# First stage of a hybrid encoder layer: x loaded first, modulation sums of the first block on TensorE, later sums spread

## The chip, the cores and the metric

The kernel runs on one core of one Trainium2 chip. The metric is the device time of one execution in microseconds (us), the median of several runs. Each engine (TensorE = PE with its weight loads PEld, VectorE = DVE, ScalarE = ACT, GpSimd = POOL, SyncE = SP) works through its own queue in order.

## The reference, cut to what matters

One encoder layer, 512 positions by 2048 features, float32. What bears on the change is its first step:

```python
c_act = silu(c)                                  # 2048 values
mod = c_act @ w_ada[l] + b_ada[l]                # w_ada: 2048 x 12288
sh1, sc1, gt1, sh2, sc2, gt2 = split(mod, 6)
h = rms_norm(x, g_norm1[l]) * (1 + sc1) + sh1    # 512 x 2048
proj = h @ w_in[l]
...
```

After it come two kinds of attention, an output projection, a second modulated norm and a SwiGLU feed-forward network. They are not touched.

## The kernel before, in words

The products are made in two-part float32: every operand is split into `hi` (fp32r) and `lo` (the rest), and a product is three matmuls (hi by hi, hi by lo, lo by hi; `mm3`, lines 240 to 243).

The input projection runs over the 16 feature slices (kc, 128 features each) in five blocks, `BLOCKS = ((0, 2), (2, 2), (4, 4), (8, 4), (12, 4))`: first slice and number of slices. In each of the first four blocks five heads are multiplied (`head_block`, line 497); the partial sums of a head stay in SBUF (`raw_in`, copied by ACT at L506 in the first block, added by DVE at L508 later). A head needs a weight chunk of 128x768 for every two slices: loaded by SP (L77), split by ACT (L89, hi) and DVE (L97, lo). So a chunk feeds 24 matmuls of 384 columns, the first two blocks have five chunks each, the next two ten each. In this text the blocks are called the first to the fifth, and the chunks are counted with them.

Before a block can start, its slices of h must exist: hT[kc] = (hh, hl). For that the scale and shift of the block (G1, SH1) are needed, and these are sums over the 2048 rows of w_ada. `ada_pair` makes them: it loads w_ada in tiles of 512 KB into `araw` (five buffers) and lets DVE add them up row by row (L334 and L336: a tile times a column of c, added to `adaacc`). There are 8 tiles and 16 instructions of 128x512 for a block of two slices, 16 tiles and 16 instructions of 128x1024 for a block of four. `ada_columns` then sums over the partitions with TensorE (L347, one-column products with `ones`, each appearing as two instructions in the trace), and DVE makes G1 and SH1 (L348 to L350). For each slice x, already divided by its norm, is transposed by TensorE (L398), ACT applies G1 and SH1 (L400) and makes hh (L401), and DVE makes hl (L402).

Order: TensorE's instructions run in the order in which the program writes them. The other engines' queues are ordered by the compiler, near the program's order. `LOADS` interleaves the tiles of the first block's sums with the loads of x. Before the first block starts, the sums of the second are loaded and added too. During a block the sums of the block after the next are made (`ahead`) and, from `NEAR` on, the columns and transposes of the next (`near`).

Of the kernel before, what the change touches and what calls it, by code (L numbers as in the profile page):

```python
# [10 lines left out]
F32 = mybir.dt.float32  # L11
F32R = mybir.dt.float32r
AF = mybir.ActivationFunctionType
ALU = mybir.AluOpType
# [4 lines left out]
P = 128  # L19
D = 2048  # L20
S = 512
NT = S // P
KC = D // P
# [12 lines left out]
N_SLOTS = 45  # L36
T2_BUFS = 4
FIRST = 5
NEAR = 0.2
LOADS = "aaaxxxxaxxxxaxxxxaxxxxwaa"  # L40
BLOCKS = ((0, 2), (2, 2), (4, 4), (8, 4), (12, 4))
PARTS = (2, 4, 4, 4, 4, 4)
STRAIGHT = 2
# [155 lines left out]
def hybrid_layer(ctx, tc, a, out):  # L199
    nc = tc.nc  # L200
    act, dve, pool, pe, sp = nc.scalar, nc.vector, nc.gpsimd, nc.tensor, nc.sync

    w_ada = a["w_ada"][0].rearrange("(p q) n -> p q n", q=KC)
    b_ada = a["b_ada"]
    x = a["x"][0]
# [14 lines left out]
    W = Weights(nc, wp, weight_plan(a))  # L220

    def slot(name, dt=F32R):
        return big.tile([P, S], dt, tag="A", bufs=N_SLOTS, name=name)

    def bank(tag, name):
        return psum.tile([P, 512], F32, tag=tag, name=name)

    turn, spare = [0], ["tmp"]
# [5 lines left out]
    def f(ap):  # L234
        return ap.bitcast(F32)

    def tsl(t):
        return slice(t * P, (t + 1) * P)
# [7 lines left out]
    ident = const.tile([P, P], F32, name="ident")  # L246
    sp.dma_start(out=ident, in_=a["ident"])
    c_col = const.tile([P, KC], F32, name="c_col")
    sp.dma_start(out=c_col, in_=a["c"][0].rearrange("(p q) -> p q", q=KC))
    act.activation(c_col, c_col, AF.Silu)  # L250
    ones = const.tile([P, 1], F32, name="ones")
# [25 lines left out]
    def scol(c, n=1):  # L277
        return small[:, c:c + n]

    anti = const.tile([P, P], F32, name="anti")  # L280
    G1 = const.tile([P, KC], F32, name="G1")
    SH1 = const.tile([P, KC], F32, name="SH1")
# [35 lines left out]
                    yield None  # L318
            sums.append(acc)

    def ada_pair(raws, accs, p_scale, p_shift, k0, nk, sums):

        n = nk * P
        acc = accs()[:, :2 * n].rearrange("p (s n) -> p s n", s=2)
        nq = 512 // n
        both = w_ada[:, :, p_shift * D:(p_scale + 1) * D].rearrange("p q (s n) -> p q s n", s=2)
        for j in range(KC // nq):
            raw = raws()[:, :2 * nq * n].rearrange("p (q s n) -> p q s n", q=nq, s=2)
            for i in range(nq):
                sp.dma_start(out=raw[:, i], in_=both[:, nq * j + i, :, k0 * P:k0 * P + n])  # L330
            for i in range(nq):
                q = nq * j + i
                if q == 0:
                    dve.tensor_scalar(out=acc, in0=raw[:, i], scalar1=c_col[:, 0:1], scalar2=None, op0=ALU.mult)  # L334
                else:
                    dve.scalar_tensor_tensor(out=acc, in0=raw[:, i], scalar=c_col[:, q:q + 1], in1=acc, op0=ALU.mult,  # L336
                                             op1=ALU.add)
            yield None
        sums += [acc[:, 1], acc[:, 0]]

    def ada_columns(sums, k0, nk, G, SH, cg, cbs, cbh):

        ks = slice(k0, k0 + nk)
        ps = bank(spare[0], "ps_ada")
        for i, acc in enumerate(sums):
            for m in range(nk):
                pe.matmul(ps[:, i * nk + m:i * nk + m + 1], acc[:, tsl(m)], ones, start=True, stop=True)  # L347
        dve.tensor_tensor(out=G[:, ks], in0=ps[:, 0:nk], in1=scol(cbs + k0, nk), op=ALU.add)  # L348
        dve.tensor_tensor(out=G[:, ks], in0=G[:, ks], in1=scol(cg + k0, nk), op=ALU.mult)
        dve.tensor_tensor(out=SH[:, ks], in0=ps[:, nk:2 * nk], in1=scol(cbh + k0, nk), op=ALU.add)  # L350
# [19 lines left out]
    def raws0():  # L370
        return st[1].tile([P, 1024], F32, tag="araw", bufs=5, name="araw")
# [6 lines left out]
    xs = [[slot("xs", F32) for _ in range(4)] for _ in range(NT)]  # L378
    hT = [None] * KC

    last_hh = [None]
    sums1 = {k0: [] for k0, _ in BLOCKS}

    def modulation_sums(k0, nk):
        yield from ada_pair(raws0, accs0, 1, 0, k0, nk, sums1[k0])

    def modulation(k0, nk):
        for b in range(1, 4):
            if k0 <= 4 * b - 2 < k0 + nk:
                with tc.issue_after(last_hh[0]):  # L390
                    for t in range(NT):
                        act.activation(xs[t][b], xs[t][b], AF.Copy, scale=rstd1[:, t:t + 1])
        ada_columns(sums1[k0], k0, nk, G1, SH1, C_G1, C_BSC1, C_BSH1)
        yield None
        for kc in range(k0, k0 + nk):
            ps = bank(spare[0], "ps_x")
            for t in range(NT):
                pe.transpose(ps[:, tsl(t)], xs[t][kc // 4][:, tsl(kc % 4)], ident)  # L398
            xt, hh, hl = slot("xt", F32), slot("hh"), slot("hl")
            act.activation(xt, ps, AF.Identity, scale=G1[:, kc:kc + 1], bias=SH1[:, kc:kc + 1])  # L400
            last_hh[0] = act.copy(out=hh, in_=xt).ins  # L401
            dve.tensor_tensor(out=hl, in0=xt, in1=f(hh), op=ALU.subtract)  # L402
            hT[kc] = (hh, hl)
            yield None

    first = modulation_sums(*BLOCKS[0])
    i = 0
    for kind in LOADS:
        if kind == "a":
            next(first)  # L410
        elif kind == "w":
            W.split(0)
        else:
            t, b = divmod(i, 4)
            sp.dma_start(out=xs[t][b], in_=x[t * P:(t + 1) * P, b * 512:(b + 1) * 512])
            i += 1

    ps = bank("tmp", "ps_small")
    pe.transpose(ps[:, :N_FIRST], stage[:N_FIRST, :], ident[:N_FIRST, :N_FIRST])
# [36 lines left out]
    for t in range(NT):  # L456
        if t % 2:
            act.activation(xs[t][0], xs[t][0], AF.Copy, scale=rstd1[:, t:t + 1])
        else:
            dve.tensor_scalar(out=xs[t][0], in0=xs[t][0], scalar1=rstd1[:, t:t + 1], scalar2=None, op0=ALU.mult)  # L460


    def raw_tile(name="raw_in"):
        return sh[1].tile([P, 384], F32, tag="rin", bufs=16, name=name)
# [32 lines left out]
    def head_block(h, k0, nk, tag, fine=False):  # L497

        pss = [bank(tag, "ps_in") for _ in range(NT)]
        yield from project(pss, hT, 384, [("in", h, j) for j in range(k0 // 2, (k0 + nk) // 2)], k0, nk,  # L500
                           fine=fine)
        if k0 == 0:
            raw_in[h] = [raw_tile() if h < 4 else slot("raw_s", F32)[:, :384] for _ in range(NT)]
        for t in range(NT):
            if k0 == 0:
                act.copy(out=raw_in[h][t], in_=pss[t][:, :384])  # L506
            else:
                dve.tensor_tensor(out=raw_in[h][t], in0=raw_in[h][t], in1=pss[t][:, :384], op=ALU.add)  # L508
# [35 lines left out]
            dve.tensor_copy(out=vec[0:H, :], in_=ps[0:H, :])  # L544
            sp.dma_start(out=vecd[:, i * 512:(i + 1) * 512], in_=vec[0:H, :])

    for gen in (first, modulation(*BLOCKS[0]), modulation_sums(*BLOCKS[1])):
        for _ in gen:
            pass
    def run(gen, total, at, start, end):  # L550

        n = total * min(1.0, max(0.0, (at - start) / (end - start)))
        while gen[1] < n:
            gen[1] += 1
            next(gen[0], None)

    for i, (k0, nk) in enumerate(BLOCKS):
        final = i + 1 == len(BLOCKS)
        ahead = [modulation_sums(*BLOCKS[i + 2]) if i + 2 < len(BLOCKS) else iter(()), 0]
        near = [iter(()) if final else modulation(*BLOCKS[i + 1]), 0]  # L560
        heads = range(1 if final else FIRST)
        for h in heads:
            tag = next_tag()
            spare[0] = "tmp" if tag == "acc" else "acc"
            for j, _ in enumerate(head_block(h, k0, nk, tag)):
                at = (h + j / nk) / len(heads)
                run(ahead, 16, at, 0.0, 0.9)
                run(near, 7, at, NEAR, 0.95)
        for gen in (ahead[0], near[0]):
            for _ in gen:  # L570
                pass
        if i == 1:
            load_small()
            load_bias()
        if i == 2:
            use_small()
            lambda_scale()
            bias_strips()
# [412 lines left out]
    diffs, heads = [DiffHead(0)], []  # L991
# [7 lines left out]
    for h in range(H):  # L999
        cur = diffs[h]  # L1000
        for step in DIFF_STEPS.split():
            kind, i = step[0], int(step[1:] or 0)
# [20 lines left out]
    for g in range(H + 1):  # L1023
# [4 lines left out]
        for step in MLA_STEPS.split():  # L1028
            kind, i = step[0], int(step[1:] or 0)
# [61 lines left out]
    due = 0.0  # L1091
    for b in range(4):
        tag = next_tag()
# [7 lines left out]
        for i, _ in enumerate(project(pss, mixT, 512, [("out", b, j) for j in range(j0, 8)], 2 * j0, KC - 2 * j0,  # L1101
                                      first=(b > 0))):
# [5 lines left out]
            if b == 1 and i % 2 and i < 16:  # L1108
                b2, t = 2 + i // 8, i % 8 // 2
# [246 lines left out]
    for u in range(N_UNITS):  # L1356
        res = unit(u)
        if u % 2 == 0:
            g = res
            act.activation(g, g, AF.Silu)  # L1360
        else:
            ao = wp.tile([P, 1024], F32, tag="raw", bufs=3, name="ao").rearrange("p (c s) -> p c s", c=4)
            dve.tensor_tensor(out=ao, in0=g, in1=res, op=ALU.mult)
            j = u // 2 + STRAIGHT
            sp.dma_start(out=actd[2 * j:2 * j + 2].rearrange("f p s -> p f s"),
                         in_=ao.rearrange("p (f c) s -> p f (c s)", f=2))
# [3 lines left out]
    sums = [[fd[1].tile([P, 512], F32, tag="sums", bufs=16, name="sums") for _ in range(4)] for _ in range(NT)]  # L1370
# [22 lines left out]
    W = Wd  # L1393
    n_parts = len(PARTS)
    j = 0
    for i, n in enumerate(PARTS):
        for b in range(4):
            tag = next_tag()
# [13 lines left out]
            for t in range(NT):  # L1412
                s = sums[t][b]
# [74 lines left out]
```

## Time and profile before

| | us |
|---|---|
| median of 3 runs | 2294.44 (2291.91 to 2295.82) |
| the profiled execution, own time | 2292.43 |
| its span, first to last instruction | 2290.6 |
| PE busy | 2183.1 (95%) |
| DVE busy | 1625.7 (71%) |

The profile is of one execution. Its time is its span plus 1.8 us around it, and it lies 2.0 us below the median. A matmul's busy time covers its passage through the array, so consecutive matmuls overlap in the records: the distance between starts is what one costs.

### The profile page before, as it was taken

How to read it: one execution, taken by the hardware profiler on the slowest of the kernel's cores; microseconds unless marked ns; L12 is line 12 of the kernel's file. 1: busy time of each engine (PE TensorE's matmuls, PEld its weight loads, DVE VectorE, ACT ScalarE, POOL GpSimd, SP SyncE). 2: the span in 40 equal slices, each digit the busy share in tenths (PEclk: the TensorE clock that was granted, in tenths of full speed). 3: DMA queues.
4: the chain of work that ended last, by engine and by line, in shares of the span. 5: the costliest groups of instructions: out<-in, count | busy, mean ns of one | idle time of the engine just before them, and what ended most of it. 6: DMA issues, size and time to landing. Idle time of an engine off the chain costs nothing.

```text
span 2290.6 us, 35353 instructions
## 1 busy us (share of the span) xinstructions
PE 2183.1 (95%) x13878; PEld 1999.4 (87%) x13878; DVE 1625.7 (71%) x2290; ACT 945.3 (41%) x1569; POOL 418.2 (18%) x478
## 2 busy tenths in 40 slices
PE   2899999998989998999999999999999999999999
PEld 2799989997777776889999999999999877888887
DVE  5987788868998477857777777777777577232543
ACT  4423545556555323434444444444444522222221
POOL 0002533436444431000000000000000122222221
PEclk9899999999999998999999999999999999999999
DMA  9975345432433577233333333333333686242542
GB/s 295 330 224 152 92 146 157 136 90 84 161 121 119 173 251 256 85 128 120 130 120 123 110 127 117 119 116 129 120 127 123 218 274 215 101 133 98 165 138 101
DMA packets 270826, 344.99 MB, mean 151 GB/s; under 512 B 15006, under 2 KB 171143, under 8 KB 270531
## 3 DMA queue, kind: packets, MB, share of 16 engines
q1 hardware_dynamic: 267864, 338.18, 45.0%
q10 hardware_dynamic: 2794, 4.55, 0.6%
q8 instruction: 108, 1.77, 0.3%
q14 instruction: 60, 0.48, 0.1%
HBM read 322.71 MB, written 19.96 MB: 150 GB/s over the span
## 4 chain that ended last, share of the span: by engine, by line
PE 60%; DVE 8%; DMA 5%; issue 2%; ACT 1%; SPq 0%; POOL 0%; DVEq 0%; ACTq 0%; POOLq 0%
PE ps_d L243 6%; PE ps_d L242 6%; PE ps_d L241 6%; PE ps_X L1253 5%; PE ps_X L1254 5%; PE ps_X L1255 5%; PE ps_W L1253 3%; PE ps_W L1255 3%; PE ps_W L1254 3%; DVE adaacc L308 3%; DMA araw<-in_w_ada_dram 2%; DMA x<-in_w_ada_dram 2%; PE ps_Z L1253 2%; PE ps_Y L1253 2%; PE ps_Y L1255 2%
## 5 line engine op out<-in xcount | busy, mean ns | idle before, releaser
L89 ACT CAST hi<-raw 128x1024 fp32r<-128x1024 f32 (+2 forms) x228 | 221.3, 971 | 494.5 <-PE ps_d L242 275.1
L97 POOL TENSOR_TENSOR lo<-raw,hi 128x1024 fp32r<-128x1024 f32 (+1 forms) x67 | 161.4, 2410 | 1386.0 <-DMA raw<-in_w_down_dram 879.9
L97 DVE TENSOR_TENSOR lo<-raw,hi 128x1024 fp32r<-128x1024 f32 (+2 forms) x161 | 178.7, 1110 | 168.3 <-ACT hi L89 164.3
L1236 ACT CAST wh<-wr 128x1024 fp32r<-128x1024 f32 x160 | 168.6, 1054 | 242.1 <-PE ps_X L1254 68.3
L1255 PE MATMUL ps_X<-comb,wl 128*128 128x256 f32 x960 | 267.8, 279 | 0.0
L1253 PE MATMUL ps_X<-comb,wh 128*128 128x256 f32 x960 | 267.8, 279 | 0.0
L1254 PE MATMUL ps_X<-comb,wh 128*128 128x256 f32 x960 | 267.8, 279 | 0.0
L243 PE MATMUL ps_d<-lo,ax 128*128 128x512 f32 x640 | 250.4, 391 | 7.6 <-DVE lo L97 7.6
L242 PE MATMUL ps_d<-hi,ax 128*128 128x512 f32 x640 | 249.6, 390 | 0.0
L241 PE MATMUL ps_d<-hi,ax 128*128 128x512 f32 x640 | 249.6, 390 | 0.0
L1219 DVE TENSOR_TENSOR wl<-wr,wh 128x1024 fp32r<-128x1024 f32 x160 | 195.5, 1222 | 74.1 <-ACT wh L1236 73.9
L243 PE MATMUL ps_in<-lo,hh 128*128 128x384 f32 (+2 forms) x704 | 232.7, 331 | 10.9 <-DVE lo L97 10.8
L241 PE MATMUL ps_in<-hi,hh 128*128 128x384 f32 (+2 forms) x704 | 238.0, 338 | 3.5 <-ACT hi L89 2.6
L242 PE MATMUL ps_in<-hi,hl 128*128 128x384 f32 (+2 forms) x704 | 232.0, 330 | 0.8 <-DVE hl L402 0.7
L1236 ACT CAST wh<-wt 128x1024 fp32r<-128x1024 f32 x120 | 126.1, 1051 | 195.2 <-PE ps_X L1254 118.8
L1219 DVE TENSOR_TENSOR wl<-wt,wh 128x1024 fp32r<-128x1024 f32 x120 | 146.7, 1223 | 78.8 <-ACT wh L1236 78.8
L1254 PEld LDWEIGHTS ps_X<-comb,wh 128*128 128x128 f32 x960 | 180.5, 188 | 0.0
L1253 PEld LDWEIGHTS ps_X<-comb,wh 128*128 128x128 f32 x960 | 180.5, 188 | 0.0
L1255 PEld LDWEIGHTS ps_X<-comb,wl 128*128 128x128 f32 x960 | 180.5, 188 | 0.0
L1253 PE MATMUL ps_W<-comb,wh 128*128 128x256 f32 x640 | 178.9, 280 | 0.9 <-DVE cu L1264 0.8
L1255 PE MATMUL ps_W<-comb,wl 128*128 128x256 f32 x640 | 178.5, 279 | 0.0
L1254 PE MATMUL ps_W<-comb,wh 128*128 128x256 f32 x640 | 178.5, 279 | 0.0
(320 smaller groups left out, 5488.7 us busy)
## 6 DMA issues: line engine op xcount, KB each, us to landing
raw<-in_w_down_dram SPq DMA_DIRECT2D x88, 512.0 KB
araw<-in_w_ada_dram SPq DMA_DIRECT2D x80, 512.0 KB
wr<-in_w_gate_dram SPq DMA_DIRECT2D x40, 1024.0 KB
wr<-in_w_up_dram SPq DMA_DIRECT2D x40, 1024.0 KB
ada<-in_w_ada_dram SPq DMA_DIRECT2D x128, 256.0 KB
raw<-in_w_in_dram SPq DMA_DIRECT2D x128, 192.0 KB
raw<-in_w_out_dram SPq DMA_DIRECT2D x32, 512.0 KB
x<-in_w_ada_dram SPq DMA_DIRECT2D x64, 256.0 KB
```

The lines of the kernel that those rows point to most:

```text
L89: nc.scalar.copy(out=hi[:, :n], in_=raw[:, :n])
L97: e.tensor_tensor(out=lo[:, :n], in0=raw[:, :n], in1=hi[:, :n].bitcast(F32), op=ALU.subtract)
L241: pe.matmul(o, ah, bh, start=start, stop=False)
L242: pe.matmul(o, al, bh, start=False, stop=False)
L243: pe.matmul(o, ah, bl, start=False, stop=stop)
L308: dve.scalar_tensor_tensor(out=acc[:, :width], in0=raw[:, i, :width], scalar=c_col[:, q:q + 1], in1=acc[:, :width], op0=ALU.mult, op1=ALU.add)
L1219: dve.tensor_tensor(out=out, in0=x, in1=y, op=ALU.subtract)
L1236: act.copy(out=hi, in_=src)
L1253: pe.matmul(ps[bk], wh[:, k], c[:, 0], start=first and k == 0, stop=False, skip_group_check=True)
L1254: pe.matmul(ps[bk], wh[:, k], c[:, 1], start=False, stop=False, skip_group_check=True)
L1255: pe.matmul(ps[bk], wl[:, k], c[:, 0], start=False, stop=k == 7, skip_group_check=True)
```

## The change

The 16 loads of x come first; the 8 tiles of the first block's sums follow. Those sums are no longer made by DVE: each 128x128 piece of a tile is the stationary operand of a TensorE product with the column of c, all into one PSUM bank (64 products). The first block's transposes stand in TensorE's order ahead of the last tile's products. The first two weight chunks are split and the third is loaded behind the tiles in the program. For the first block ACT makes hh directly from PSUM while DVE makes xt.

Of the second block's 16 rows DVE adds 8; the other 8 go to TensorE in `ada_columns` (`DVE_ROWS`), so their four `araw` buffers are held until then. The sums and the columns of later blocks are issued at points given in nominal microseconds of projection work (`SUMS`, `MODS`): a block's sums are now spread over the block ahead of it, not the one before that.

```diff
-NEAR = 0.2
-LOADS = "aaaxxxxaxxxxaxxxxaxxxxwaa"
+SUMS = ((0.0, 12.5), (13.0, 35.0), (36.0, 66.0), (67.0, 104.0))
+DVE_ROWS = {2: 8}
+MODS = ((13.0, 19.0), (35.0, 39.0), (66.5, 77.0), (104.5, 116.0))
...
+                if q >= n_dve:
+                    rest.append(((raw[:, i, 1], raw[:, i, 0]), c_col[:, q:q + 1]))
+                elif q == 0:
...
     def ada_columns(sums, k0, nk, G, SH, cg, cbs, cbh):
+        ps = bank(spare[0], "ps_ada")
+        terms = [(sums[:2], ones)] + sums[2:]
+        for j, (pair, col) in enumerate(terms):
+            for i, part in enumerate(pair):
+                for m in range(nk):
+                    pe.matmul(ps[:, i * nk + m:i * nk + m + 1], part[:, tsl(m)], col, start=j == 0 and i == 0 and m == 0,
+                              stop=j + 1 == len(terms), skip_group_check=True)
+        gain_and_shift(ps, k0, nk, G, SH, cg, cbs, cbh)
...
+    def evacuate(kc, ps, both):
+        xt, hh, hl = slot("xt", F32), slot("hh"), slot("hl")
+        if both:
+            last_hh[0] = act.activation(hh, ps, AF.Identity, scale=G1[:, kc:kc + 1], bias=SH1[:, kc:kc + 1]).ins
+            dve.tensor_scalar(out=xt, in0=ps, scalar1=G1[:, kc:kc + 1], scalar2=SH1[:, kc:kc + 1], op0=ALU.mult,
+                              op1=ALU.add)
...
+    for i in range(16):
+        t, b = divmod(i, 4)
+        sp.dma_start(out=xs[t][b], in_=x[t * P:(t + 1) * P, b * 512:(b + 1) * 512])
...
+    for j in range(KC // nq):
+        raw = raws0().rearrange("p (q s n) -> p q s n", q=nq, s=2)
+        for i in range(nq):
+            sp.dma_start(out=raw[:, i], in_=both[:, nq * j + i, :, k0 * P:(k0 + nk) * P])
+        for i in range(nq):
+            q = nq * j + i
+            for c in range(2 * nk):
+                pe.matmul(ps0[:, c:c + 1], raw[:, i, 1 - c // nk, tsl(c % nk)], c_col[:, q:q + 1],
+                          start=q == 0 and c == 0, stop=q == KC - 1, skip_group_check=True)
+        if j == KC // nq - 2:
+            spare[0] = "acc"
+            psx = [turned(kc) for kc in range(k0, k0 + nk)]
+    W.split(0)
+    W.split(1)
+    W.load(2)
+    gain_and_shift(ps0, k0, nk, G1, SH1, C_G1, C_BSC1, C_BSH1)
+    for i in range(nk):
+        evacuate(k0 + i, psx[i], True)
...
+    side1 = [[paced(modulation_sums(k0, nk), 4 * nk + 2, s), paced(modulation(k0, nk), nk + 2, m)]
+             for (k0, nk), s, m in zip(BLOCKS[1:], SUMS, MODS)]
     for i, (k0, nk) in enumerate(BLOCKS):
...
+            for us in head_block(h, k0, nk, tag):
+                for pair in side1:
+                    for g in pair:
+                        run(g, at)
+                at += us
```

## Rows read from the trace of the kernel before

**Rows 1.** The page, busy time of each engine.

```profile
PE 2183.1 (95%) x13878; PEld 1999.4 (87%) x13878; DVE 1625.7 (71%) x2290; ACT 945.3 (41%) x1569; POOL 418.2 (18%) x478
```

**Rows 2.** Busy time in windows; at the end granted clock, DMA share, GB/s.

```profile
0.00:20.00 20.00, 0.31 (x1) 0.18 (x1) 6.24 (x12) 6.91 (x15) 0.20 (x4) 1.00 0.77 237
20.00:41.00 21.00, 3.67 (x16) 3.27 (x16) 10.38 (x19) 10.82 (x27) 1.21 (x2) 1.00 1.04 341
71.00:106.00 35.00, 29.48 (x152) 28.07 (x152) 32.94 (x43) 12.60 (x18) 0.00 (x0) 0.85 0.98 316
159.00:206.00 47.00, 47.00 (x276) 45.25 (x277) 25.96 (x49) 16.05 (x22) 4.75 (x7) 1.00 0.47 127
...
78.00:85.00 7.00, 6.13 (x20) 6.13 (x21) 6.12 (x8) 0.83 (x1) 0.00 (x0) 0.52 1.08 349
```

**Rows 3.** Waits of PE, 41 to 206 us: total, times, longest.

```profile
PE ps_in L243 <- DVE lo L97: 10.8, 4, 5.1
```

**Rows 4.** Timeline around the first block's start: start, duration, instruction, idle before.

```profile
36.81 1.78 PEld L347 LDWEIGHTS ps_ada<-ones,adaacc 128*128 128x128 f32 x8 [32.71 <-DVE adaacc L336]
...
38.54 1.95 PE L398 MATMUL ps_x<-ident,xs 128*128 128x128 f32 x8
...
38.91 0.16 DVE L349 TENSOR_TENSOR G<-G,small 128x2 f32<-128x2 f32 x1
...
39.67 0.78 ACT L400 ACTIVATE xt<-ps_x,SH,G 128x512 f32<-128x512 f32 x1 [5.52 <-PE ps_x L398]
...
41.15 0.69 PE L241 MATMUL ps_in<-hi,hh 128*128 128x384 f32 x1 [0.67 <-ACT hh L401]
```

**Rows 5.** Timeline of PE, 44 to 88 us.

```profile
44.02 0.69 PE L242 MATMUL ps_in<-hi,hl 128*128 128x384 f32 x1 [0.72 <-DVE hl L402]
...
46.74 0.52 PE L241 MATMUL ps_in<-hi,hh 128*128 128x384 f32 x1
...
47.49 0.34 PE L241 MATMUL ps_in<-hi,hh 128*128 128x384 f32 x1
...
85.50 1.84 PE L347 MATMUL ps_ada<-ones,adaacc 128*128 128x1 f32 x16
87.20 0.42 PE L241 MATMUL ps_in<-hi,hh 128*128 128x384 f32 x1
```

**Rows 6.** Timeline, rows that mark ends of blocks and chunks.

```profile
71.03 0.48 ACT L506 COPY raw_s<-ps_in 128x384 f32<-128x384 f32 x1 [0.33 <-PE ps_in L243]
...
111.71 0.69 PE L243 MATMUL ps_in<-lo,hh 128*128 128x384 f32 x1 [5.08 <-DVE lo L97]
...
158.85 0.83 ACT L89 CAST hi<-raw 128x768 fp32r<-128x768 f32 x1 [3.32 <-PE ps_in L242]
...
188.73 0.83 ACT L89 CAST hi<-raw 128x768 fp32r<-128x768 f32 x1 [2.44 <-PE ps_in L242]
193.34 0.83 ACT L89 CAST hi<-raw 128x768 fp32r<-128x768 f32 x1 [2.44 <-PE ps_in L242]
...
202.10 0.84 ACT L89 CAST hi<-raw 128x768 fp32r<-128x768 f32 x1 [3.32 <-DVE ada L308]
206.26 0.84 ACT L89 CAST hi<-raw 128x768 fp32r<-128x768 f32 x1 [3.32 <-PE ps_in L242]
```

**Rows 7.** Timeline, a small load's issue and the instruction that waits for it.

```profile
2.11 0.42 SPq L271 DMA_DIRECT2D stage<-in_b_ada_dram  x1
...
3.95 0.31 PE L419 MATMUL ps_small<-ident,stage 48*128 48x48 f32 x1 [3.95 <-DMA stage<-in_b_ada_dram]
```

**Rows 8.** Groups of DVE by shape, 41 to 206 us: busy, mean ns.

```profile
L336 DVE SCALAR_TENSOR_TENSOR adaacc<-araw,c_col,adaacc 128x1024 f32<-128x1024 f32 x45 | 57.5, 1278 | 1.1 <-DMA araw<-in_w_ada_dram 0.9
L97 DVE TENSOR_TENSOR lo<-raw,hi 128x768 fp32r<-128x768 f32 x30 | 28.6, 958 | 9.8 <-ACT hi L89 9.1
L508 DVE TENSOR_TENSOR raw_in<-raw_in,ps_in 128x384 f32<-128x384 f32 x48 | 25.7, 548 | 5.2 <-PE ps_in L243 5.0
L402 DVE TENSOR_TENSOR hl<-xt,hh 128x512 fp32r<-128x512 f32 x16 | 11.0, 686 | 2.4 <-ACT hh L401 2.3
```

More of the change, by code (lines that the diff above doesn't have):

```diff
@@ L319, in ada_sums, with ada_pair @@
             sums.append(acc)
-    def ada_pair(raws, accs, p_scale, p_shift, k0, nk, sums):
+    def ada_pair(raws, accs, p_scale, p_shift, k0, nk, sums, n_dve=KC):
         n = nk * P
         acc = accs()[:, :2 * n].rearrange("p (s n) -> p s n", s=2)
-        nq = 512 // n
+        nq, rest = 512 // n, []
         both = w_ada[:, :, p_shift * D:(p_scale + 1) * D].rearrange("p q (s n) -> p q s n", s=2)
@@ L332, in ada_pair @@
                 q = nq * j + i
-                if q == 0:
+                if q >= n_dve:
+                    rest.append(((raw[:, i, 1], raw[:, i, 0]), c_col[:, q:q + 1]))
+                elif q == 0:
                     dve.tensor_scalar(out=acc, in0=raw[:, i], scalar1=c_col[:, 0:1], scalar2=None, op0=ALU.mult)
@@ L338, in ada_pair, with gain_and_shift @@
             yield None
-        sums += [acc[:, 1], acc[:, 0]]
+        sums += [acc[:, 1], acc[:, 0]] + rest
     def ada_columns(sums, k0, nk, G, SH, cg, cbs, cbh):
+        ps = bank(spare[0], "ps_ada")
[6 more added lines that the diff above has]
+        gain_and_shift(ps, k0, nk, G, SH, cg, cbs, cbh)
+    def gain_and_shift(ps, k0, nk, G, SH, cg, cbs, cbh):
         ks = slice(k0, k0 + nk)
[L344 to L347, printed above, removed]
         dve.tensor_tensor(out=G[:, ks], in0=ps[:, 0:nk], in1=scol(cbs + k0, nk), op=ALU.add)
@@ L384, in modulation_sums, with turned @@
     def modulation_sums(k0, nk):
-        yield from ada_pair(raws0, accs0, 1, 0, k0, nk, sums1[k0])
+        yield from ada_pair(raws0, accs0, 1, 0, k0, nk, sums1[k0], DVE_ROWS.get(k0, KC))
+    def evacuate(kc, ps, both):
[4 more added lines that the diff above has]
+                              op1=ALU.add)
+        else:
+            act.activation(xt, ps, AF.Identity, scale=G1[:, kc:kc + 1], bias=SH1[:, kc:kc + 1])
+            last_hh[0] = act.copy(out=hh, in_=xt).ins
+        dve.tensor_tensor(out=hl, in0=xt, in1=f(hh), op=ALU.subtract)
+        hT[kc] = (hh, hl)
+    def turned(kc):
+        ps = bank(spare[0], "ps_x")
+        for t in range(NT):
+            pe.transpose(ps[:, tsl(t)], xs[t][kc // 4][:, tsl(kc % 4)], ident)
+        return ps
     def modulation(k0, nk):
@@ L395, in modulation @@
         for kc in range(k0, k0 + nk):
[L396 to L403, printed above, removed]
-            yield None
[L406 to L416, printed above, removed]
+            evacuate(kc, turned(kc), False)
+            yield None
+    for i in range(16):
+        t, b = divmod(i, 4)
+        sp.dma_start(out=xs[t][b], in_=x[t * P:(t + 1) * P, b * 512:(b + 1) * 512])
     ps = bank("tmp", "ps_small")
@@ L460, in hybrid_layer @@
             dve.tensor_scalar(out=xs[t][0], in0=xs[t][0], scalar1=rstd1[:, t:t + 1], scalar2=None, op0=ALU.mult)
+    k0, nk = BLOCKS[0]
+    both = w_ada[:, :, 0:2 * D].rearrange("p q (s n) -> p q s n", s=2)
+    ps0 = bank("tmp", "ps_ada0")
+    nq = 4 // nk
+    for j in range(KC // nq):
[16 more added lines that the diff above has]
+        evacuate(k0 + i, psx[i], True)
     def raw_tile(name="raw_in"):
@@ L545, in bias_strips, with paced, run @@
             sp.dma_start(out=vecd[:, i * 512:(i + 1) * 512], in_=vec[0:H, :])
[L547 to L555, printed above, removed]
+    def paced(gen, n, span):
+        return [gen, n, 0, span]
+    def run(g, at):
+        gen, n, done, (start, end) = g
+        due = n * min(1.0, max(0.0, (at - start) / (end - start)))
+        while g[2] < due:
+            g[2] += 1
+            next(gen, None)
+    at = 0.0
+    side1 = [[paced(modulation_sums(k0, nk), 4 * nk + 2, s), paced(modulation(k0, nk), nk + 2, m)]
+             for (k0, nk), s, m in zip(BLOCKS[1:], SUMS, MODS)]
     for i, (k0, nk) in enumerate(BLOCKS):
         final = i + 1 == len(BLOCKS)
[L559 to L562, printed above, removed]
+        for h in range(1 if final else FIRST):
             tag = next_tag()
             spare[0] = "tmp" if tag == "acc" else "acc"
[L565 to L571, printed above, removed]
+            for us in head_block(h, k0, nk, tag):
[3 more added lines that the diff above has]
+                at += us
+        if not final:
+            for g in side1.pop(0):
+                for _ in g[0]:
+                    pass
         if i == 1:
```

## The prediction

> **What bounds the kernel now.** I read the page first, then windows over the first 206 us, then PE's waits and the timeline at the block borders. PE is busy 95% of the span [rows 1], so time can only come from where it is not: 41 us ahead of the first projection matmul [rows 2, 4], and the first three blocks, which wait. The marks: the first block starts at 41.15 [rows 4] and ends when its last copy is released, about 71.0; the third starts at 106.1 (its third matmul, at 111.71, sat 5.08 us waiting for a `lo`; the two ahead of it end at 106.6); the fourth starts about 158.8 and ends about 206.2, when PE's L242 releases the next `hi` [rows 6]. So the blocks take 29.9, 35.1, 52.7 and 47.4 us.
>
> What would they take at full speed? One chunk is 4.16 us (202.10 to 206.26); with one slice's four transposes 4.61 (188.73 to 193.34), so those are 0.45 [rows 6]. Sixteen one-column instructions take 1.70 (85.50 to 87.20), 0.106 each [rows 5]. The second block is 5 x 4.16 + 1.70 + 4 x 0.45 = 24.3, the third 41.6 + 3.5 = 45.1; the fourth runs at its content already. So some 10.8 us are lost in the second block and 7.6 in the third. DVE is the reason: busy 32.94 of 35 us there, PE waits 10.8 us for its `lo` [rows 2, 3], and after such waits matmuls run at half speed (granted clock 0.52 in 78 to 85, the 1.2 GHz level) [rows 2]. Behind 206 us the sequence is the same before and after; I carry a shift at that mark to the end unchanged.
>
> **The change, part by part. (1) x first.** 4.2 MB of x and 0.2 MB of small loads at the 237 GB/s of the first 20 us are in by about 18.5; the first tile (0.52 MB at 341 GB/s: 1.5 us) by about 20.2 [rows 2]. The loads are the same bytes in another order, 16 of x past 16 of w_ada in SP's queue; the 16 loads of the second block's sums, issued ahead of the first block until now, come behind three chunks and have until 71, when some 15 MB must have landed (by 51 at these rates); what moves is that sums can start at 20.2 and the norm is off the path (its scaled x is done well before the transposes).
>
> **(2) The first block's sums on PE.** This removes 16 DVE instructions from the path and adds 64 products, 128 instructions of PE. At which clock? PE has been idle until then. The nearest row is the same form after idle: 8 instructions keep the weight loads busy 1.78 us, 0.2225 each [rows 4], twice the 0.106 above [rows 5]. There too PE worked without a gap from 36.81 to about 40.5 on one-column products and transposes, and the next matmuls were still at half speed: 0.52 long up to 46.74, 0.34 from 47.49 on, after 3 us of dense 384-column work [rows 4, 5]. (The windows [rows 2] read a clock of 1.00 there, but no change of clock had been recorded yet; the spacing tells.) Bounds: 128 x 0.106 = 13.6 and 128 x 0.2225 = 28.5 us. I take 28.5, the row nearest in what came before it. A tile then takes 3.56 us on PE against 1.5 to load, so PE, not DMA, sets the pace, and the five buffers don't bind. Transposes are 1.95 [rows 4]: the sums end at 20.2 + 28.5 + 1.95 = 50.6. G1 follows 0.5 later (38.59 to 39.07), hh by one ACT instruction of 0.78 [rows 4]: the first matmul starts at about 51.9, 10.8 later than before.
>
> Here the Trainium skill (TensorE: Matmul & The Clock Gate, section LDWEIGHTS) bears on it: a weight load takes its number of columns over 1.2 GHz, 107 ns for 128, whatever the product's width. So it too says that a one-column product pays a full weight load; but 128 x 0.107 is 13.7 us where the row gives 28.5. By the page the result would be about that of rival A. The row decides here, being this form after idle; the sum doesn't use the page.
>
> **(3) Chunks split early, hh without the second step.** Two chunks are in place before the block, so the waits for chunk two and three at its start go. The start costs 0.5 for the first hl and, at half speed, about 2.2 until dense work has brought the clock back (44.02 to 47 [rows 5]: 3 us, so 1.5 lost, behind a thinner start from 41.15 on). I count 2.7.
>
> **(4) Half of the second block's sums on PE.** `ada_columns` becomes 9 x 4 products, 72 instructions: 7.65 us of PE time in the first block at 0.106, up to 16.0 at 0.2225; I take 7.65, since dense work runs up to them. It is bare cost on PE. The first block is 20.8 + 0.9 + 7.65 + 2.7 = 32.05 and ends at 84.0, 13 later than before.
>
> **(5) Later sums spread.** The third block's sums, 16 DVE instructions, were made a block earlier and ready long before. Now they are issued in the first block's last heads and the second, and their columns stand in PE's order half a head before the second block's end. Four of five `araw` buffers are held by the rows left to PE, which reach PE at 51.9 + 2.7 + 4 x 4.16 = 71.2; the first is free 24 instructions later, 73.8. SP waits there with the tile's load, and the weight loads behind it. A load needs 1.84 us at least (2.11 to 3.95) [rows 7] and 1.5 for the bytes: the second tile is there at 77.2. DVE then has, up to the columns, 15 sums of 1.28, six `lo` of 0.96, 16 additions of 0.55 and two hl of 0.69: 35.1 us by the means [rows 8], about 32 if starts overlap the end before by 0.08. I take 32: done at 109.2. PE reaches the columns at 84.0 + 18.7 = 102.7 and waits 6.5 us; behind it in PE's order lie the last half head and the next block's transposes, and ACT waits for these. Then 1.7 + 2.1 + 1.35 and about 1 us of G1 and hh that nothing covers any more: the second block ends at about 115.4 (before: 106.1). DMA allows it: 16 tiles and six chunks, 11 MB, need 32 us at 341 GB/s.
>
> The third block has then its sums' DVE work (13 x 1.28 + 4 heads of 4.1 + 2.7, 36 us) inside the 36 us up to its columns: no wait, 45.5 us, end at 160.9 (before 158.8). The gain is here: the 5.08 wait and the half-speed stretch behind it are gone. In the fourth, DVE takes over some 14 us of sums on top of 25.96 in 47 [rows 2]: covered, with up to 3 us of waits for `lo`, of which I take 1.
>
> Sum: +10.8 (start) + 2.2 (first block) - 3.7 (second: 31.4 for 35.1) - 7.2 (third) + 1.0 = +3.1 us. The profiled execution would go from 2292.4 to 2295.5; with its 2.0 below the median, 2297.5.
>
> **The rivals.** *A: the sums run at 2.4 GHz.* If one-column products alone raise the clock, some 22 instructions (5 us, about what passed from 41.15 to the rise [rows 5]) run at 0.2225 and 106 at 0.106: 16.1 instead of 28.5, and the transposes 1. The first matmul starts at about 38.6, and without the slow start the first block ends at 68.5. The chain of part 5 then runs from 55.8 + 2.55 + 3.35 + 32 = 93.7 and the second block ends at 99.9; the third at 145.4; with the fourth -12.4: 2282. For it: no row shows one-column work alone for long (1.78 us of it, then transposes). Against: the same stretch as read above [rows 4]. It ends on the other side and decides alone.
>
> *B: slower by DVE's order.* At half speed as in the forecast, but `lo` queues in DVE behind sums that wait for their tiles, now that tiles come just in time: one such wait cost 5.1 us [rows 3], plus up to 2.8 of half speed behind it. Or the 72 instructions of part 4 drop to half speed: 8.4 more, of which 2.6 reach the first buffer's release and so the chain, plus a slow restart. Either gives +4 to +9: 2301 to 2307.
>
> *C: the early part costs nothing at the end,* since DVE's chain gives way (DVE idles early and takes sums sooner than I count): the 6.5 us wait shrinks to 2; 2293.
>
> **How the numbers follow.** About 0.2% (4.6 us) is what a measurement of this kernel can tell. Forecast 0.27 (0.15 of it within 0.2%, 0.12 slower); C 0.15 (0.11 within, 0.04 faster). A: 0.32, nearly all faster (0.29). B: 0.26, slower. So faster 0.33, same 0.29, slower 0.38. The forecast's own range is 2290 to 2301; the range reaches to A and B: 2279 to 2306.
>
> **What the next profile would show.** Right: PEld rows of the first sums at about 0.22 each, back to back from 20 to 50; the first `ps_in` matmul near 52; an idle PE of 5 to 8 us ahead of the third block's L347-like columns, released by DVE `adaacc`; the third block in about 45 us. Wrong: those weight loads at 0.11 from 25 us on and a first matmul before 42 (A); waits of L243 for `lo` of 5 us in the second or fourth block (B); or a shift at the mark (fourth block's end) that doesn't reach the end.

## The result, and the profile after

The changed kernel takes 2314.8 us (median of 4 runs, 2310.4 to 2316.3) against 2295.1 for the kernel before (4 runs on the same chip): a ratio of 1.008, 95% interval 1.006 to 1.0099. It is slower by 19.7 us, and outside the range of 2279 to 2306.

The page's row of busy times answers to [rows 1]: PE is busy 44 us longer, and for a share of the span that is no smaller; DVE is busy 22.5 us less.

```profile
PE 2227.1 (96%) x14062; PEld 2043.5 (88%) x14062; DVE 1603.2 (69%) x2268; ACT 943.6 (41%) x1567; POOL 420.7 (18%) x478
```

The windows of the first stage, cut at the block borders, answer to [rows 2]. Columns: window, length, busy time of PE, PEld, DVE, ACT, POOL, then granted clock, DMA share, GB/s.

```profile
20.00:50.50 30.50, 28.51 (x135) 28.42 (x134) 1.93 (x6) 2.84 (x5) 0.92 (x1) 1.00 0.66 189
50.50:92.00 41.50, 39.29 (x194) 38.29 (x195) 15.80 (x24) 15.85 (x28) 0.00 (x0) 0.84 0.73 222
92.00:127.00 35.00, 29.87 (x160) 27.97 (x158) 31.26 (x43) 11.40 (x18) 0.00 (x0) 0.90 0.83 264
...
73.30:76.00 2.70, 2.70 (x27) 2.70 (x25) 0.00 (x0) 1.21 (x2) 0.00 (x0) 1.00 0.78 228
78.00:85.00 7.00, 7.00 (x35) 7.00 (x34) 0.00 (x0) 0.00 (x0) 0.00 (x0) 0.50 0.61 201
```

In the first of these stretches, 30.5 us, DVE is nearly idle (1.93 us) and PE is full: the sums have changed engines. In the first block DVE still has little to do (15.80 of 41.5) and PE, busy 39.29, is the bound. The last two rows are cut out of that block and are read below.

The timeline of PE shows what fills it (start, duration, instruction, idle before); it answers to [rows 4] and [rows 5].

```profile
19.47 24.02 PE L489 MATMUL ps_ada<-c_col,araw 128*128 128x1 f32 x112 [15.14 <-ACT sq L468]
43.35 1.95 PE L414 MATMUL ps_x<-ident,xs 128*128 128x128 f32 x8
45.09 3.41 PE L489 MATMUL ps_ada<-c_col,araw 128*128 128x1 f32 x16
50.55 0.69 PE L244 MATMUL ps_in<-hi,hh 128*128 128x384 f32 x1 [2.04 <-ACT hi L92]
52.14 0.69 PE L245 MATMUL ps_in<-hi,hl 128*128 128x384 f32 x1 [0.90 <-DVE hl L408]
...
54.73 0.69 PE L245 MATMUL ps_in<-hi,hl 128*128 128x384 f32 x1 [1.26 <-DVE hl L408]
...
59.69 0.52 PE L245 MATMUL ps_in<-hi,hl 128*128 128x384 f32 x1
...
60.47 0.34 PE L245 MATMUL ps_in<-hi,hl 128*128 128x384 f32 x1
...
73.33 0.94 PE L354 MATMUL ps_ada<-ones,adaacc 128*128 128x1 f32 x8
74.13 10.93 PE L354 MATMUL ps_ada<-c_col,araw 128*128 128x1 f32 x64
84.92 0.67 PE L244 MATMUL ps_in<-hi,hh 128*128 128x384 f32 x1
...
90.40 0.52 PE L246 MATMUL ps_in<-lo,hh 128*128 128x384 f32 x1
...
91.19 0.33 PE L246 MATMUL ps_in<-lo,hh 128*128 128x384 f32 x1
```

The counts are of instructions, two to a one-column product: the 64 products of the first block's sums are 112 and 16 of them, and `ada_columns` has 8 and 64. Three things are to be read here. The first 112 take 24.02 us, 0.2145 each, without a gap: half speed for all that time, and the first projection matmul stands at 50.55 instead of 41.15. The matmuls behind it stay 0.52 long until 60. And the 64 new instructions in the first block take 10.93 us, 0.17 each, which lies between the 0.10 of the eight just ahead of them (73.33 to 74.13) and the 0.2145 of the start. The clock falls inside the run: the windows above have it granted in full (1.00) from 73.3 to 76 and at 0.50, the 1.2 GHz level, from 78 to 85. The 384-column matmuls behind the run are 0.52 long until 90.7.

The rows that mark the block ends (a `hi` that waits for the block's last chunk) answer to [rows 6].

```profile
92.43 0.84 ACT L92 CAST hi<-raw 128x768 fp32r<-128x768 f32 x1 [0.99 <-PE ps_in L245]
...
175.15 0.83 ACT L92 CAST hi<-raw 128x768 fp32r<-128x768 f32 x1 [0.48 <-PE ps_in L245]
...
222.59 0.84 ACT L92 CAST hi<-raw 128x768 fp32r<-128x768 f32 x1 [0.48 <-PE ps_in L245]
```

The third block's first matmul is at 127.2 (its row stands with part 5 below). So the blocks take 41.9, 34.8, 47.9 and 47.5 us, where the sum had 32.05, 31.4, 45.5 and 48.4. The mark, the end of the fourth block, is at 222.6 instead of 206.3: 16.3 us later, where 3.1 were forecast. The profiled executions differ by 22.0 at the end (2314.4 and 2292.4), the medians by 19.7.

PE's waits, 0 to 223 us, answer to [rows 3] (total, times, longest):

```profile
PE ps_in L246 <- DVE lo L100: 3.5, 3, 2.6
PE ps_in L245 <- DVE hl L408: 2.7, 4, 1.3
PE ps_in L244 <- ACT hi L92: 2.0, 1, 2.0
PE ps_ada L354 <- DVE adaacc L342: 0.8, 1, 0.8
```

The waits for `lo` fell from 10.8 to 3.5 us, as the sum said of the spreading. The wait of 6.5 us at the columns, which part 5 placed ahead of the third block, is 0.8.

### The profile page after: what moved, and what is told of

It is laid out like the page before. It is cut to its first block, busy times and chain, and to the rows that moved or that the text cites. A ratio compares the mean times of both kernels' runs of the same rounds, so it can differ in the third digit from the quotient of the medians.

```text
span 2312.6 us, 35687 instructions
## 1 busy us (share of the span) xinstructions
PE 2227.1 (96%) x14062; PEld 2043.5 (88%) x14062; DVE 1603.2 (69%) x2268; ACT 943.6 (41%) x1567; POOL 420.7 (18%) x478
## 4 chain that ended last, share of the span: by engine, by line
PE 54%; DMA 4%; DVE 4%; issue 1%; ACT 1%; POOL 0%; SPq 0%; DVEq 0%; ACTq 0%; POOLq 0%
PE ps_d L246 6%; PE ps_d L244 6%; PE ps_d L245 5%; PE ps_X L1295 4%; PE ps_X L1296 4%; PE ps_X L1297 4%; PE ps_W L1295 3%; PE ps_W L1297 3%; PE ps_W L1296 3%; DVE adaacc L311 2%; DMA araw<-in_w_ada_dram 2%; PE ps_Z L1295 2%; PE ps_Z L1297 1%; PE ps_Z L1296 1%; PE ps_Y L1295 1%; PE ps_Y L1296 1%
```

## The experiments

The theory after the result: the spreading gains, and each of the two sets of one-column products costs its own PE time, most of it at half clock, with a slow restart behind it; the two prices add. The rival: one of the two, or the spread order itself, spoils the second block, and the products are only its neighbours. Every ratio below is to the kernel before on the same chip, with its 95% interval; the medians of the kernel before there were 2296.2 (e1 to e4), 2295.6 (e5 to e8) and 2295.6 (e9, e10).

**e1: the second block's sums back on DVE.**

```diff
-DVE_ROWS = {2: 8}
+DVE_ROWS = {}
```

> All 16 rows of the second block's sums are added by DVE again; all else as in the changed kernel. Theory T (one-column products run at 1.2 GHz, and a long run of them also takes the clock from the dense work behind it): the stretch of 72 one-column instructions, 11.6 us, shrinks to 8 of 0.9, and the 2.8 us lost behind it at half speed go; the first block ends some 13 us sooner, near 79, and the time falls by 8 to 13 us, to about 2304. Theory R (the loss is in the later sums, made just in time: DVE and the tile buffers): the first block ends sooner, but 8 more sums on DVE make the second block wait as much longer; time within 4 us of the changed kernel, 2311 to 2318.

Measured: 2296.65 us, ratio 1.0004 [0.9994, 1.0013]; 18.2 us under the changed kernel, where theory T had 8 to 13. In the first block only the eight instructions of the columns are left:

```profile
72.99 0.95 PE L354 MATMUL ps_ada<-ones,adaacc 128*128 128x1 f32 x8
```

No 0.52-long matmul follows them, and the first block ends at 78.5 instead of 92.4, after a start (51.17) that is the same within 0.7. The mark is at 209.8, 12.8 ahead of the changed kernel's. At the mark theory T's size holds, and theory R, which had the second block wait longer by as much, is out: part 4 costs about 14 us in the first block, and what it takes off DVE gives back 1.2 in the second (36.0 us in e1, 34.8 in the changed kernel).

**e2: the first block's sums back on DVE, the second's still half on PE.**

```diff
-    for j in range(KC // nq):
...
-                pe.matmul(ps0[:, c:c + 1], raw[:, i, 1 - c // nk, tsl(c % nk)], c_col[:, q:q + 1],
...
+    for _ in modulation_sums(k0, nk):
+        pass
...
+    ada_columns(sums1[k0], k0, nk, G1, SH1, C_G1, C_BSC1, C_BSH1)
```

> The first block's sums are added by DVE as before, behind the loads of x; the rows of the second block stay on TensorE, the later sums stay spread. Theory T: the last tile lands near 31, DVE keeps pace (1.5 us for a tile), the first projection matmul starts near 35 instead of 50.6, and the time falls by about 13 to 16 us, to about 2300. Theory R: the start is as early, but later blocks wait for their sums, since these are limited by DMA and DVE; the shift shrinks to under 6 us by the end of the second block and the time is 2309 or more.

Measured: 2300.83 us, 1.0024 [1.0012, 1.0036]; 14.0 under the changed kernel, within theory T's 13 to 16. The first matmul is at 37.29. The 64 instructions of part 4 fall to half speed here as well:

```profile
59.45 0.34 PE L246 MATMUL ps_in<-lo,hh 128*128 128x384 f32 x1
59.63 0.94 PE L354 MATMUL ps_ada<-ones,adaacc 128*128 128x1 f32 x8
60.44 11.94 PE L354 MATMUL ps_ada<-c_col,araw 128*128 128x1 f32 x64
72.23 0.67 PE L244 MATMUL ps_in<-hi,hh 128*128 128x384 f32 x1
...
75.58 0.52 PE L245 MATMUL ps_in<-hi,hl 128*128 128x384 f32 x1
```

What is to be seen: 0.34 ahead of the run, 0.52 behind it, and no gap between. The clock has fallen inside the run.

**e3: all sums on DVE; x first, hh direct and the spreading stay.** This is e1 and e2 together.

> Both: no sums on TensorE but the columns; what is left of the change is x first, hh made directly, and the later sums spread. Theory T: the two savings add up, about 26 us, to about 2289, faster than the kernel before by some 6 us. Theory R: 2305 or more, since the spreading alone costs what the kernel before did not pay.

Measured: 2284.24 us, 0.9953 [0.9936, 0.997]. It is faster than both kernels, and by some 5 us faster than theory T's 2289. The first matmul is at 37.15, the first block ends at 65.0, the mark is at 194.0, 12.3 ahead of [rows 6]. Against it, the first block's products alone cost 12.4 us (e1), part 4 alone 16.6 (e2), both 30.6 (the changed kernel): 29.0 and 30.6 agree within the scatter, so the two prices add. Which of them is the higher is not told: by the mark the first is 15.8 us and the second 13.7.

**e4: the changed kernel with the clock held up.** 48 dense 512-column matmuls on a constant go ahead of the first block's sums and three behind each row of them; they add work to PE and nothing to the output.

```diff
+    def keep_busy(n):
+        for _ in range(n):
+            pe.matmul(ps_d0, ones_r, dense, start=True, stop=True)
+    keep_busy(48)
...
+            keep_busy(3)
```

> The changed kernel with dense matmuls added whose results are not used: 48 of 512 columns ahead of the first tile and 3 behind each of the 16 rows of the first block's sums. Theory T: the one-column products then take 0.107 us an instruction instead of 0.2145; with the 48 added dense matmuls (0.22 each, 10.6 us) the sums end some 4 us sooner than in the changed kernel, and the first block starts at full speed, 3 to 5 us more: time 2306 to 2310. Theory L (a weight load of float32 from a tile that a DMA has just written takes 0.21 whatever the clock): the products stay at 0.21, the added work comes on top, the first block starts some 10 us later, and the time is 2322 or more.

Measured: 2311.59 us, 1.0068 [1.0051, 1.0086].

```profile
17.17 4.05 PE L488 MATMUL ps_dense<-dense,ones_r 128*128 128x512 f32 x17
21.07 0.95 PE L498 MATMUL ps_ada<-c_col,araw 128*128 128x1 f32 x8
21.87 0.94 PE L488 MATMUL ps_dense<-dense,ones_r 128*128 128x512 f32 x3
...
48.11 0.44 PE L244 MATMUL ps_in<-hi,hh 128*128 128x384 f32 x1 [0.51 <-ACT hh L402]
50.43 0.69 PE L245 MATMUL ps_in<-hi,hl 128*128 128x384 f32 x1 [1.87 <-DVE hl L408]
```

Eight instructions go by in 0.80 us (21.07 to 21.87), 0.10 each instead of 0.2145: the price of 0.2145 is the clock's, and theory L is out. The fillers take nearly as much again, so the first matmul is only 2.4 us earlier than in the changed kernel, and behind the stall at the block's start (1.87 for the first `hl`) the matmuls are 0.52 long again. The full-speed start that theory T counted on didn't come, and the time is 1.6 us above its range. The half clock could thus be shown, but not avoided at a profit.

The Trainium skill (TensorE: Matmul & The Clock Gate, section LDWEIGHTS) gives a weight load's nanoseconds as its number of columns over 1.2, so 107 ns for 128 columns. That agrees with the 0.10 us of this run and not with the 0.2145 of the changed kernel's start, where the measurement decides: an estimate from the page is 13.7 us for the sums' 128 instructions, and the trace has 27.4.

**e5: e3, but only every second row of the third block's sums is added** (all tiles are loaded; the rest of that block's modulation is left out).

```diff
+                if k0 == 4 and p_scale == 1 and q % 2:
+                    continue
```

> The version with all sums on DVE and the later sums spread, but of the third block's 16 rows only every second one is added (that part of the scale and shift is left out); all 16 tiles are still loaded. Theory D (the second block is as long as DVE's queue makes it: its `lo` and the sums stand in one queue): about 10 us of DVE work fall away, the waits for `lo` and the half-speed stretch in the second block go, and its 34 us (65 to 99) become 25 to 28; time 2276 to 2279. Theory M (tiles come at the rate of DMA and their buffers): the tiles still set the columns' time, the second block stays within 3 us, time 2281 to 2286.

Measured: 2282.24 us, 0.995 [0.9935, 0.9965]. With eight of DVE's 1.28 us instructions gone from the second block, the waits for `lo` are gone, but the third block starts only 2.5 us earlier (96.13 for 98.66), and PE still waits for the sums at the columns:

```profile
89.91 1.95 PE L356 MATMUL ps_ada<-ones,adaacc 128*128 128x1 f32 x16 [0.86 <-DVE adaacc L344]
```

The time is in theory M's range, though the `lo` waits went as theory D had it. The second block takes 30.7 us instead of 33.7, where its content at full speed is 24.3: half of these sums is worth 3.0 of the 9.4 us that it loses. It is one execution against one, and e7 below shows how far this block can differ between two.

**e6: e3 without the spreading,** that is with the kernel before's own loop (the second block's sums ahead of the first block, the rest by shares of a block).

```diff
-    side1 = [[paced(modulation_sums(k0, nk), 4 * nk + 2, s), paced(modulation(k0, nk), nk + 2, m)]
-             for (k0, nk), s, m in zip(BLOCKS[1:], SUMS, MODS)]
+    for _ in modulation_sums(*BLOCKS[1]):
+        pass
...
+        ahead = [modulation_sums(*BLOCKS[i + 2]) if i + 2 < len(BLOCKS) else iter(()), 0]
+        near = [iter(()) if final else modulation(*BLOCKS[i + 1]), 0]
```

> The version with all sums on DVE, x first and hh made directly, but with the old pacing: the second block's sums before the first block, each later block's sums made two blocks ahead. If the spreading is what gains (theory S): the second block's waits for `lo` are back, and the time is 2292 to 2297, as before. If the early start is what gains (theory X, x first lets the first matmul start 4 us sooner, and the chunks wait less): 2284 to 2290.

Measured: 2298.4 us, 1.0017 [1.0007, 1.0026]: all of e3's gain is gone, as theory S has it (1.4 us above its range), though the first matmul is as early as in e3, within 0.2 us. PE's waits have the row of [rows 3] back, and a wait at the second block's columns beside it:

```profile
PE ps_in L246 <- DVE lo L100: 10.9, 4, 5.3
PE ps_ada L354 <- DVE adaacc L342: 4.4, 1, 4.4
```

Both are waits for DVE. SP's queue has changed too. This is e6, 30 to 55 us (start, time SP spent on the group, instruction):

```profile
32.48 19.42 SPq L334 DMA_DIRECT2D araw<-in_w_ada_dram  x18
52.03 0.92 SPq L80 DMA_DIRECT2D raw<-in_w_in_dram  x2
```

And this is e3 over the same stretch:

```profile
31.96 2.04 SPq L334 DMA_DIRECT2D araw<-in_w_ada_dram  x4
37.15 0.90 SPq L80 DMA_DIRECT2D raw<-in_w_in_dram  x2
```

Sums that stand together bring their loads together. In e6 the next weight chunk's load stands behind 18 of them and is issued at 52.03 instead of 37.15. Little of that reaches PE there: its waits for `hi` add up to 0.5 us. In the kernel before, one such case is to be seen, at the second chunk of the second block:

```profile
62.64 6.13 SPq L330 DMA_DIRECT2D araw<-in_w_ada_dram  x4
68.82 1.00 SPq L77 DMA_DIRECT2D raw<-in_w_in_dram  x2
75.79 0.83 ACT L89 CAST hi<-raw 128x768 fp32r<-128x768 f32 x1 [4.29 <-DMA raw<-in_w_in_dram]
76.68 0.44 PE L241 MATMUL ps_in<-hi,hh 128*128 128x384 f32 x1 [1.21 <-ACT hi L89]
```

So the gain of the spreading lies in DVE's queue, where the sums no longer stand ahead of `lo` (10.8 us of waits before, 10.9 in e6, 2.9 in e3). In SP's queue the loads of the sums no longer stand ahead of the weights either, which the prediction didn't count as a gain; the rows show 1.2 us of it at PE, and no run takes the two queues apart.

**e7: e3 with 32 dense matmuls while PE waits for the first sums;** no change to the output.

```diff
+    for _ in range(32):
+        pe.matmul(ps_d0, ones_r, dense, start=True, stop=True)
```

> The version with all sums on DVE, and 32 dense matmuls whose results are not used between the first transposes and the first columns, where TensorE sat idle for 9.9 us. Theory T (clock): the columns take 0.9 instead of 1.87 us, and the first chunk, 9.8 us for 4.2 of content, runs at full speed between its waits: 3 to 4 us less, time near 2281. If what delays the first chunk is only its waits for hl (theory H), at most 1 us less: 2283 to 2285.

Measured: 2284.83 us, 0.996 [0.9949, 0.9971], as e3. The columns are fast now, but behind the waits that follow them the matmuls are 0.52 long again until 46:

```profile
34.42 1.05 PE L354 MATMUL ps_ada<-ones,adaacc 128*128 128x1 f32 x8 [1.95 <-DVE adaacc L342]
36.80 0.69 PE L244 MATMUL ps_in<-hi,hh 128*128 128x384 f32 x1 [1.32 <-ACT hh L402]
39.11 0.69 PE L245 MATMUL ps_in<-hi,hl 128*128 128x384 f32 x1 [1.63 <-DVE hl L408]
39.60 0.52 PE L246 MATMUL ps_in<-lo,hh 128*128 128x384 f32 x1
```

Inconclusive on what a fast start would bring at the end, since no fast start came of it. The profiled execution also shows how much the second block differs between executions: 37.0 us from its first matmul on, where e3, e9 and e10 have 33.4, with 28 half-speed matmuls for their 10, while its waits add up to no more. Its mark is 3.9 us behind e3's, though the medians are 0.6 apart.

**e8: e7, and the split of the second weight chunk moved behind `hh` and `hl`,** so that its `lo` no longer stands ahead of the first `hl` in DVE's queue.

```diff
+    W.load(1)
...
+    W.split(1)
+    W.load(2)
```

> As the run with dense matmuls while idle, and the second weight chunk is split behind the first block's hh and hl in the program, so that its lo (0.95) stands behind hl in DVE's queue. Theory H: hl comes 0.9 us sooner and the first chunk with it; 1 to 2 us below that run, 2279 to 2281. Theory T alone: the same as that run within 1 us.

Measured: 2286.19 us, 0.9962 [0.9947, 0.9977]. The waits for `hl` go from 4.3 to 4.0 us in all, and the mark is e3's (194.0). The 1 to 2 us that theory H had under e7 don't show.

**e9 and e10: the spreading alone, put into the kernel before, and e3 once more beside it.** In e9, the loop's lines of e6's diff are the other way round and the rest is the kernel before.

> The kernel before with one part of the change alone: the sums of the second to fifth block are issued by the change's schedule (SUMS, MODS, one clock over the blocks), so the second block's no longer stand ahead of the first block; the order of loads, all sums on VectorE and the evacuation in two steps stay as before. Theory S (spreading alone gains what e3 gains; x first and the direct hh give nothing at the end): first matmul at 41 as before, first block end at about 69 (before 75.8, e3 65.0 with its first matmul 4 us earlier), fourth block's end at 194 to 198 (before 206.3), 2283 to 2288, so 0.4 to 0.6% under before. Rival X (spreading needs the earlier start, since otherwise the second block's sums, begun at 41 instead of 37, come late at their columns): PE waits for adaacc by 4 us or more ahead of the second block's end, fourth block's end at 200 to 204, 2289 to 2293.

> The kernel of e3 once more (all sums on VectorE, x first, direct hh, spread), on the same chip as e9. If e3's gain holds, 2283 to 2286, 0.4 to 0.6% under before. Theory S: within 3 us of e9; rival X: 5 us or more under e9.

Measured: e9 2286.1 us, 0.9969 [0.9958, 0.998]; e10 2286.2 us, 0.9953 [0.994, 0.9966]. The first matmul of e9 is at 41.84, as before, and the mark at 196.7: 9.5 ahead of [rows 6], where e3 is 12.3 and e10 12.0 ahead. So theory S holds, and the spreading brings most of the gain without any other part: over three quarters by the marks, two thirds by the ratios (0.31 of 0.47%). Block by block, e9's first is 3.8 us shorter than the kernel before's, its second 1.6 and its third 4.8. (The first block of the kernel before ends at 71.0, as the prediction reads it; the 75.8 in e9's expectation is one chunk later.) The start that is 4.7 us earlier in e3 is worth some 2.5 at the mark, and the two medians don't tell that apart.

## Why the prediction was wrong, point by point

**The half clock at the start: right.** Part 2 took 28.5 us for the sums from the row nearest in what came before it and put the first matmul at 51.9; it is 50.55, with 27.4 us for the 128 instructions. e4 shows that the clock was the reason. Rival A, which had 0.32, is out: it had 106 of the 128 at 0.106, and the mean of the first 112 is 0.2145.

**Part 3, the slow start: 2.7 us became 6.1.** Its step "I count 2.7" took the slow stretch from the kernel before, 44.02 to 47. Here the matmuls were 0.52 long till 60.0, 9.5 us behind the first, with two waits for `hl` (0.90 and 1.26) in that stretch; behind the second wait it went on for 5.3 us, and why that is longer than before stays open. The chunks were also not in place before the block: ACT makes both `hi` behind the first `hh`, and the first matmul waits for one of them; DVE makes one `lo` ahead of each of the two `hl` (50.53 and 52.00). What these cost is open: e8 moved the second `lo` away and found 0.3 us less of waits.

```profile
48.99 0.78 ACT L402 ACTIVATE hh<-ps_x,SH,G 128x512 fp32r<-128x512 f32 x1 [26.71 <-DVE G L361]
49.67 1.55 ACT L92 CAST hi<-raw 128x768 fp32r<-128x768 f32 x2
```

The first chunk's end is 10.3 us behind its start (60.85, the `hi` that it releases), where 4.16 + 2.7 were counted.

**Part 4: the step that failed.** "I take 7.65, since dense work runs up to them." Dense work ran up to them, and by the two rates (0.10 and 0.2145) only the first eight and an estimated 26 of the 64 went at full speed. The 72 took 11.6 us (73.33 to 84.92), and 2.8 us more were lost behind them: 84.92 to 90.72 holds 15 matmuls and four transposes, which at full speed take 3.05 us (0.173 each, that is 4.16 for 24, and 0.45). That is 6.7 over the sum. It is what rival B's second half describes, half speed and a slow restart; but B let only 2.6 of its 8.4 us reach the end, since PE was to wait for DVE at the second block's columns anyway. That cover wasn't there (0.8 us of wait), so all of it reached the mark, and the range ended too low. e1 and e2 show the same price from both sides: 12.8 and, against e3, 13.7 us at the mark (207.7 and 194.0), near the 10.93 of the 64 instructions and the 2.8 behind them.

**Part 5, second block: 34.8 us for 31.4.** The chain of DVE that was to end 6.5 us late at the columns ended 0.8 late. SP was held as was worked out, by the buffers kept for TensorE's rows:

```profile
72.05 15.90 SPq L334 DMA_DIRECT2D araw<-in_w_ada_dram  x6
```

but the first block ended 8 us later than counted, and the sums had that much longer. So the total came near for another reason than the one given. What the block lost was elsewhere: 2.6 us for one `lo` that came behind a sum and additions in DVE's queue, with half-speed matmuls behind it, and again half speed behind the columns:

```profile
110.39 0.44 PE L246 MATMUL ps_in<-lo,hh 128*128 128x384 f32 x1 [2.61 <-DVE lo L100]
...
119.56 1.95 PE L354 MATMUL ps_ada<-ones,adaacc 128*128 128x1 f32 x16 [0.82 <-DVE adaacc L342]
...
124.46 0.53 PE L245 MATMUL ps_in<-hi,hl 128*128 128x384 f32 x1
...
127.23 0.44 PE L244 MATMUL ps_in<-hi,hh 128*128 128x384 f32 x1 [0.23 <-ACT hh L407]
```

Added up over the block's rows, PE's waits make 5.4 us and 22 half-speed matmuls some 3.2 (0.32 from start to start for 0.173), on 24.3 of content at full speed; some 2 us are left open. e5 took half of the third block's sums out of e3's kernel and found 3.0 us, so DVE's work is a part of the loss and not the whole.

**Third and fourth block: 47.9 and 47.5 for 45.5 and 48.4.** Direction right, 7.2 us of gain forecast and 4.8 found.

**The shift at the mark, carried unchanged: 16.3 became 19.7 by medians.** It holds within some 3 us. All eleven profiled executions (the changed kernel and e1 to e10) end later against the kernel before's than their mark says, by 1.3 to 7.1 us, 4.7 in the mean. That is mostly the execution of before itself: its 2292.4 lies 2.7 to 3.7 under the medians of its runs, and the prediction had allowed 2.0. The rest goes with no one part of the change (e1 has 1.3 and e9 2.2, e4 7.1 and e10 7.0), lies in work that no kernel here changes, and was not taken apart.

**The sum.** Forecast +3.1 at the mark; -1.35 (start), +9.8 (first block: 3.4 of part 3, 6.7 of part 4, less 0.3), +3.4 (second), +2.4 (third), -0.9 (fourth) make +16.4, where the marks have +16.3. The sign of the forecast was right. Its size failed in the first block above all: the price of the one-column instructions there was taken at the full clock, and nothing behind them covered what they cost beyond it.

**Rival C,** that the early part costs nothing at the end, is out as well: e1 and e2 have the early products' time in full at the mark.

## What to carry to other kernels

Don't price a long run of one-column products at the full clock because dense work runs up to it. Here runs of 8 and 16 instructions right behind full-speed matmuls took 0.10 and 0.106 each, but of 72 about half went at the slower clock, with slow matmuls behind them, and 128 behind an idle stretch all did. A sum that DVE does beside PE's work was cheaper here than the same sum on the engine that bounds the kernel. Spreading side work over the preceding block takes bursts out of each queue that it issues to, so look at what stands behind a burst in SP's queue as well as in DVE's. And when a change has parts, run each alone: here one part gains 0.3 to 0.6% (e9 alone; e3 against e6), and two others cost 0.5 to 0.7% each.

## What the runs showed of the hardware that was not expected

In a run of 72 one-column instructions right behind full-speed matmuls the granted clock fell to its lower level (1.2 GHz) on the way, in the changed kernel, e2 and e4 alike: 10.93, 11.94 and 11.41 us for the same 64, between 6.4 at 0.10 each and 13.7 at 0.2145. PE's records show no gap in that time (in the changed kernel busy 2.70 of 2.70 us from 73.3, at a clock of 1.00, and 7.00 of 7.00 from 78, at 0.50): here the clock fell without an idle stretch ahead of it. The windows' granted clock didn't show the half speed of the start (it reads 1.00 from 20 to 50.5); the durations of the instructions did.
